# A first stage rebuilt: modulation on two engines, squares summed on TensorE

## The chip, the core and the metric

The kernel runs on one core of a Trainium2 chip. A core has TensorE (PE, matrix products; its weight loads are listed apart as PEld), VectorE (DVE), ScalarE (ACT), GpSimd (POOL) and SyncE (SP), which issues the loads. SBUF is the working memory, PSUM takes the matrix products. The metric is the device time of one execution in microseconds (us): 1756.03 us, the median of 3 runs (1755.61 to 1757.57).

## The reference

Two transformer-like blocks follow each other over 512 tokens of 1024 features. The change lies in the very first lines of the first block, the modulated norm and the projection behind it:

```python
c_act = jax.nn.silu(c)                               # c: one row of 1024
mod = c_act @ w_ada + b_ada                          # 1024 -> 3 x 1024
shift, scale, gate = jnp.split(mod, 3, axis=-1)
h = rms_norm(x, norm_in_gain) * (1.0 + scale) + shift
proj = h @ w_in                                      # q, k, v, z_attn, xbc, dt, z_ssm
```

rms_norm divides each token by the root of the mean of its squared features (plus 1e-6) and multiplies with a gain for each feature. Behind it come stick-breaking attention, a causal convolution with silu over the channels xbc, a chunked state-space scan, an out-projection scaled by gate, then a feed-forward layer, retention and pooling, a second feed-forward layer and a last norm. Nothing of these is touched, except that the weights for gate come under another name.

## The kernel before

Activations lie feature-major: a tile holds 128 features on the partitions and 512 tokens along the free axis, so x is eight tiles x0[0..7], and k counts the blocks of 128 features. A large product is taken as three float32r passes over operands split exactly in two, h and l: W.h times x.h, W.l times x.h, W.h times x.l. A float32r matmul with 512 columns is one instruction. A plain float32 matmul, as in the sums of columns, is two instructions.

TensorE's instructions run in the order in which the program writes them (`manual_schedule`). The other engines' order is made by a planner, which places an instruction where its inputs are ready by its own estimate; where the kernel wants another order, it adds a dependence with `after(later, earlier)`. All loads are issued by SP, in a single queue: a load that waits for a buffer holds those behind it.

The first stage, lines 313 to 400, does this:

- Loads (L344 to L350): x0[0], x0[1], the row c, x0[2..7], the vector table vec, the table cm. Then the rows of w_ada for shift and scale, 512 KB each for each k, and the first projection's weights wst[k], 384 KB each. For k above 0 these loads carry a dependence on the last square.
- Squares and their sum (L362 to L376): ACT squares each x0[k]. DVE adds the eight squares up. TensorE sums over the partitions with four matmuls of one column each (`colsum`, L252). DVE and POOL take the root, `rc` (L376); `bcast` (L272) spreads it as a row over all partitions: DVE makes a diagonal `dg`, TensorE multiplies it with ones into `Rp` in PSUM.
- silu(c): the row c is spread over the partitions by two matmuls with one row (L359), and ACT takes silu from PSUM into `cact`.
- Modulation (L322 to L342): for each k, shift and scale are two DVE instructions of 1024 elements that multiply 128 rows of w_ada with `cact` and sum up. `sh` and `gs` are made from these by two narrow ones.
- The loop over k (L383 to L400): POOL multiplies x0[k] with Rb, the copy of Rp in SBUF. ACT makes `hxh` with scale gs and bias sh. DVE makes the same in full precision (L395) and subtracts for `hxl` (L113). The weights are split by ACT (L132) and POOL (L133; for k = 1 DVE). TensorE multiplies six blocks in three passes, 18 matmuls for each k, into six PSUM banks `start_ps`.
- `warmup(n)` (L315) issues n matmuls of ones into a bank that nobody reads: 12 at the start, 10 behind silu's broadcasts, 11 behind the column sums, 6 behind Rp.

Behind the loop a queue of projections (`adv`) keeps TensorE fed with the remaining products on hx; the convolution takes `start_ps`.

Of the kernel before, what the change touches and what calls it, by code (L numbers as in the profile page):

```python
# [30 lines left out]
# columns of the vector table  # L31
# [3 lines left out]
def _vec_layout():  # L35
    n = 0
    for name, w in (
        ("gin", 8), ("bsh", 8), ("bsc", 8), ("bgt", 8), ("cw0", 12), ("cw1", 12), ("cw2", 12),
        ("cw3", 12), ("cb", 12), ("sbg", 8), ("ssg", 8), ("gf", 8), ("g1", 8), ("gm", 8), ("gb0", 8),
        ("gb1", 8), ("ps", 8), ("g2", 8), ("gfin", 8), ("dtb", 16), ("alog", 16), ("dsk", 16),  # L40
    ):
        VEC[name] = (n, w)
        n += w
    return n
# [5 lines left out]
def program(tc, A, out):  # L50
    """Activations lie feature-major [128 features, 512 tokens]; every large product is taken as three
    float32r passes over operands split exactly in two (h + l). TensorE runs in program order: `adv`
    interleaves the queue of projections with the products of attention, SSD and retention."""
# [71 lines left out]
    def wload(ap, n, dep=None, order=None, eng=None):  # L125
        r = wr.tile([P, 1024], F32, tag="wr", name=nm("wr"))
        d = SP.dma_start(r[:, :n], ap)
        if dep is not None:
            after(d, dep)
        h = wh.tile([P, 1024], F32R, tag="wh", name=nm("wh"))  # L130
        l = wl.tile([P, 1024], F32R, tag="wl", name=nm("wl"))
        i = ACT.copy(h[:, :n], r[:, :n])  # L132
        j = (eng or DVE).tensor_sub(l[:, :n], r[:, :n], h[:, :n].bitcast(F32))  # L133
        if order is not None:
            after(i, order[0])
            after(j, order[1])
        return h, l

    class Stream:
        """A projection's weights, in chunks of eight 128 x 128 blocks in the order of their use."""  # L140
# [16 lines left out]
    # ---------------------------------------------------------------- the queue of projections  # L157
# [6 lines left out]
    def adv(n=10**9):  # L164
        """Emit about n k-steps of the queued projections; the next one's first weights are asked for early."""
        while n > 0 and queue:
            job = queue[0]
            try:
                n -= next(job.steps)
            except StopIteration:  # L170
                queue.popleft()
                continue
            job.left -= 1
            if job.left == AHEAD and len(queue) > 1:
                queue[1].ahead()
# [9 lines left out]
    def proj(stream, xs, fin):  # L185
        """[128 features, 512 tokens] = stream's next blocks x xs."""
# [16 lines left out]
    def modeb(aps, n, xs, fin, side=None):  # L203
        """Token-major product: 4 banks [128 tokens, n]; aps: per pair of k-tiles [128, 2 * n]."""
# [30 lines left out]
    # ---------------------------------------------------------------- constants  # L235
# [16 lines left out]
    def colsum(sq, more=None, cols=range(4), pc=None):  # L252
        """sums over features, as columns of tokens"""
# [18 lines left out]
    def bcast(col, order=None, copies=1):  # L272
        """columns of tokens as a row on every partition (in PSUM)"""
# [38 lines left out]
    # ---------------------------------------------------------------- first block: modulated norm  # L312
    warm = ps_("warm")

    def warmup(n):  # L315
        """keeps TensorE's clock up while the first operands are made"""
# [4 lines left out]

    def matvec(src, col, dep=None, pool=(wr, "wr")):  # L322
        """col = rows of src (128 features x 1024) times silu(c)"""
        w = pool[0].tile([P, D], F32, tag=pool[1], name=nm("wa"))
        d = SP.dma_start(w, src)
        if dep is not None:
            after(d, dep)
        return DVE.scalar_tensor_tensor(w, w, 1.0, cact, op0=ALU.mult, op1=ALU.mult, accum_out=col)  # L328

# [3 lines left out]
    scaled = {}  # L333

    def modulation(k, dep=None, order=None):
        first = matvec(A["ada"][0, k], mv[:, k : k + 1], dep)
        second = matvec(A["ada"][1, k], mv[:, 8 + k : 9 + k], dep, (wh, "wh"))
        if order is not None:
            after(first if k else second, order)
        DVE.tensor_add(sh[:, k : k + 1], mv[:, k : k + 1], V("bsh", k))  # L340
        scaled[k] = DVE.scalar_tensor_tensor(gs[:, k : k + 1], mv[:, 8 + k : 9 + k], bsc1[:, k : k + 1], V("gin", k), op0=ALU.add, op1=ALU.mult)
        return first, second  # L342

    x0 = [a(F32, "x") for _ in range(KD)]  # L344
    for k in range(KD):
        SP.dma_start(x0[k], A["xT"][k])
        if k == 1:
            SP.dma_start(crow, A["c"])
    SP.dma_start(vec, A["vec"])
    SP.dma_start(cm, A["cm"])  # L350
    # one table for silu, square and copies
# [3 lines left out]
    cact = const([P, D], "cact")  # L355
    silus = []
    for n in range(2):
        pb = ps_("pb")
        mm(pb, ones[0:1, :], crow[:, 512 * n : 512 * n + 512], True, True)  # L359
        silus.append(ACT.activation(cact[:, 512 * n : 512 * n + 512], pb, AF.Silu))  # L360
    warmup(WARM[1])
    sq = None  # L362
    for k in range(KD):
        s = k_(F32, "sq")
        last = ACT.activation(s, x0[k], AF.Square)
        if k == 7:
            for i in silus:
                after(i, last)
        sq = accum(sq, s)
    DVE.tensor_scalar(bsc1, V("bsc"), 1.0, None, op0=ALU.add)  # L370
    pc = colsum(sq)
    warmup(WARM[2])
    rt = small([P, 4], "rct")
    order = DVE.tensor_scalar(rt, pc, 1.0 / D, EPS, op0=ALU.mult, op1=ALU.add)
    rc = small([P, 4], "rc")
    POOL.tensor_tensor(rc, rt, mhalf, op=ALU.pow)  # L376
    Rp = bcast(rc, modulation(0, order=order))
    scaled0 = DVE.tensor_tensor(x0[0], x0[0], Rp, op=ALU.mult)
    Rb = a(F32, "rb")
    after(ACT.copy(Rb, Rp), scaled0)  # L380
    warmup(WARM[3])
    hx = []
    start_ps = [ps_("mp") for _ in range(6)]  # L383
    for k in range(KD):
        dep = last if k > 0 else None
        if k > 0:
            modulation(k, dep, order[1] if k == 1 else scaled[1])
        h, l = a(F32R, "hxh"), a(F32R, "hxl")
        gk, sk = gs[:, k : k + 1], sh[:, k : k + 1]
        if k > 0:  # L390
            POOL.tensor_tensor(x0[k], x0[k], Rb, op=ALU.mult)
        i = ACT.activation(h, x0[k], AF.Identity, bias=sk, scale=gk)  # L392
        if k == 0:
            order = (i, scaled0)
        DVE.tensor_scalar(x0[k], x0[k], gk, sk, op0=ALU.mult, op1=ALU.add)  # L395
        lo(l, x0[k], h)
        hx.append((h, l))
        w = wload(A["wst"][k], 768, dep, (order[0], scaled[k]) if k else None, POOL if k != 1 else DVE)
        for n, (i, j) in enumerate(((0, 0), (1, 0), (0, 1))):
            for m in range(6):  # L400
                mm(start_ps[m], w[i][:, m * P : (m + 1) * P], hx[k][j], k == 0 and n == 0, k == KD - 1 and n == 2)

    # ---------------------------------------------------------------- conv + silu of the SSM channels
# [17 lines left out]
    # ---------------------------------------------------------------- z_ssm and dt, token-major  # L421
# [19 lines left out]
    # values of the attention, token-major, head by head as [h | l]  # L441
    VS = [[None] * 4 for _ in range(4)]

    def gate_part(m):
        """the gate of the first block, one eighth at a time"""
        matvec(A["ada"][2, m], mv[:, 16 + m : 17 + m])
# [13 lines left out]
    # queries and keys of the attention: a head's q as [h; l] on the partitions, k as [h; h] and [l; l]  # L460
# [45 lines left out]
    # softplus(x) = max(x, 0) + log1p(e), e = exp(-|x|); log1p(e) = 2 atanh(e / (2 + e))  # L506
# [24 lines left out]
    # cumulative log decay: as columns [token, (chunk, head)] and as rows, broadcast through DRAM  # L531
# [16 lines left out]
    # ---------------------------------------------------------------- SSD  # L548
# [11 lines left out]
    def post(c):  # L560
        """gate and normalise a finished chunk"""
# [103 lines left out]
    # the SSM half of the out-projection: x + gate * (W^T y), kept in DRAM during the attention  # L665
# [13 lines left out]
    # ---------------------------------------------------------------- attention  # L679
# [104 lines left out]
    # ---------------------------------------------------------------- out-projection of the first block  # L784
# [44 lines left out]
    # ---------------------------------------------------------------- feed-forward  # L829
    ff = {}  # L830

    def ffn(xs, win, wout, norm, gnext, last=False):
        """res += 0.5 * swiglu(R * xs); norm(n) gives R in two steps; the squares and split input of the next norm."""
# [64 lines left out]
    # ---------------------------------------------------------------- mixing: retention and pooling  # L898
# [112 lines left out]
    # pooled windows (feature-major, along the tokens)  # L1011
# [3 lines left out]
    def pool_fin(ps, g):  # L1015
# [8 lines left out]
        # the first windows are shorter: their count is t + 1  # L1024
# [76 lines left out]
    # ---------------------------------------------------------------- last rows and final norm, in two halves of the tokens  # L1101
# [8 lines left out]
    def rows(hf, hook=None):  # L1110
        """the last 256 features of half the tokens, and their squares"""
# [46 lines left out]
    def others(i, k):  # L1158
        """the sums of the features before, while the first half runs"""
# [4 lines left out]
    def first(i, k):  # L1164
        """the first half's norm and output, while the second runs"""
# [131 lines left out]
```

## Time and profile before

| | |
|---|---|
| median of 3 runs | 1756.03 us |
| profiled execution | span 1756.9 us |
| granted TensorE clock, mean | 0.991 |
| PE busy | 1720.6 us, 98% |
| DVE / ACT / POOL busy | 980.6 / 662.5 / 206.0 us |
| DMA, HBM read | 174.93 MB |

The profile is one execution, taken by the hardware profiler. Times are from the first instruction. In a list of groups, a row has the line, the engine, the operation, out<-in by the program's names, the shapes and the count, then the busy time in us and the mean of one in ns, then the idle time of the engine just before, with what ended it. In order of time, a row has its start, its length, and what it is. In a table of stretches, a row has the busy time of PE, PEld, DVE, ACT and POOL with the count of instructions, then PEclk, the share of the clock that TensorE was granted, the DMA engines' share and GB/s.

### The profile page before, as it was taken

What the parts mean: (1) busy time and instruction counts of PE and PEld (TensorE: products, weight loads), DVE (VectorE), ACT (ScalarE), POOL (GpSimd) and SP (SyncE); (2) the same over time, 40 slices, a digit from 0 to 9 for tenths busy, and PEclk for the clock granted to TensorE, in tenths of its full rate; (3) what the DMA queues carried; (4) which work ended last, traced back from release to release, by engine and by line L of the source; (5) the groups of instructions that cost most, each with busy time, mean ns of one, the idle gap of its engine ahead of it and who ended that gap; (6) DMA issues with size and microseconds to landing.
All of it is one profiled execution on the core that took longest, in us unless ns stands there. A gap on an engine that the chain in (4) does not pass through costs nothing.

```text
span 1756.9 us, 20492 instructions
## 1 busy us (share of the span) xinstructions
PE 1720.6 (98%) x8034; PEld 1432.1 (82%) x8034; DVE 980.6 (56%) x1347; ACT 662.5 (38%) x1023; POOL 206.0 (12%) x250
## 2 busy tenths in 40 slices
PE   8999899999999999999999999999999999999998
PEld 6798688777877888888888888888888888888887
DVE  7956965999967334333443636762544433433334
ACT  3545553667644222222333333332433322222232
POOL 4202212344321000000000000220000100000001
PEclk8999999999999999999999999999999999999999
DMA  6536344111132223222342222222223322222221
GB/s 231 183 89 201 96 156 156 61 61 60 56 116 94 97 99 104 95 98 96 120 132 90 85 90 90 78 97 96 96 96 114 102 96 96 96 96 96 96 96 49
DMA packets 56627, 182.59 MB, mean 104 GB/s; under 512 B 6289, under 2 KB 6609, under 8 KB 56530
## 3 DMA queue, kind: packets, MB, share of 16 engines
q1 hardware_dynamic: 56530, 181.28, 31.2%
q8 instruction: 63, 1.03, 0.2%
q14 instruction: 34, 0.28, 0.1%
HBM read 174.93 MB, written 6.32 MB: 103 GB/s over the span
## 4 chain that ended last, share of the span: by engine, by line
PE 82%; DVE 9%; issue 5%; POOL 2%; ACT 1%; DMA 1%; SPq 0%; POOLq 0%; DVEq 0%; ACTq 0%
PE mp L98 69%; PE mb L98 9%; DVE wa L328 1%; DVE om L725 1%; PE sc L98 1%; POOL be L723 1%; DVE wl L133 1%; PE ro L98 1%; POOL om L723 1%; DVE be L726 1%; PE yp L98 1%; DVE KL L113 1%; DVE x L395 1%; DVE wTl L113 0%; PE pc L98 0%
## 5 line engine op out<-in xcount | busy, mean ns | idle before, releaser
L132 ACT CAST wh<-wr 128x1024 fp32r<-128x1024 f32 (+3 forms) x288 | 298.0, 1036 | 779.0 <-PE mp L98 465.0
L133 DVE TENSOR_TENSOR wl<-wr,wh 128x1024 fp32r<-128x1024 f32 (+3 forms) x281 | 343.1, 1222 | 154.2 <-PE mp L98 86.2
L98 PE MATMUL mp<-xsh,wh 128*128 128x512 f32 x1024 | 401.3, 392 | 3.2 <-ACT xsh L109 3.2
L98 PE MATMUL mp<-xsl,wh 128*128 128x512 f32 x1024 | 399.2, 390 | 0.1
L98 PE MATMUL mp<-xsh,wl 128*128 128x512 f32 x1024 | 399.1, 390 | 0.0
L98 PEld LDWEIGHTS mp<-xsh,wh 128*128 128x128 f32 x1024 | 192.6, 188 | 43.2 <-ACT xsh L109 3.7
L98 PEld LDWEIGHTS mp<-xsl,wh 128*128 128x128 f32 x1024 | 192.7, 188 | 40.6 <-DVE xsl L114 0.6
L98 PEld LDWEIGHTS mp<-xsh,wl 128*128 128x128 f32 x1024 | 192.5, 188 | 40.4
L98 PE MATMUL mp<-aah,wh 128*128 128x512 f32 (+1 forms) x374 | 141.2, 377 | 0.0
L98 PE MATMUL mp<-aah,wl 128*128 128x512 f32 (+1 forms) x374 | 140.8, 377 | 0.0
L98 PE MATMUL mp<-aal,wh 128*128 128x512 f32 (+1 forms) x374 | 140.8, 376 | 0.0
L849 DVE TENSOR_TENSOR g<-g,mp 128x512 f32<-128x512 f32 x44 | 30.3, 688 | 155.4 <-PE mp L98 153.4
L98 PE MATMUL mp<-hxh,wh 128*128 128x512 f32 x288 | 112.5, 414 | 4.5 <-ACT hxh L392 4.5
L98 PE MATMUL mp<-hxh,wl 128*128 128x512 f32 x288 | 108.6, 400 | 0.8 <-POOL wl L133 0.8
L98 PE MATMUL mp<-hxl,wh 128*128 128x512 f32 x288 | 107.6, 396 | 1.0 <-DVE hxl L113 0.9
L309 POOL TENSOR_TENSOR ssq<-sq,sq 128x512 f32<-128x512 f32 x6 | 9.0, 1506 | 825.2 <-ACT sq L300 811.9
L847 DVE TENSOR_TENSOR g<-mp,rb 128x512 f32<-128x512 f32 x44 | 30.4, 692 | 118.4 <-PE mp L98 118.0
L98 PEld LDWEIGHTS mp<-aal,wh 128*128 128x128 f32 x374 | 70.4, 188 | 13.0
L98 PEld LDWEIGHTS mp<-aah,wh 128*128 128x128 f32 x374 | 70.4, 188 | 12.9
L98 PEld LDWEIGHTS mp<-aah,wl 128*128 128x128 f32 x374 | 70.4, 188 | 12.8
L98 PEld LDWEIGHTS mp<-hxh,wh 128*128 128x128 f32 x288 | 55.1, 193 | 17.3 <-ACT hxh L392 6.8
L98 PEld LDWEIGHTS mp<-hxh,wl 128*128 128x128 f32 x288 | 55.0, 192 | 14.9 <-POOL wl L133 2.8
(294 smaller groups left out, 2778.5 us busy)
## 6 DMA issues: line engine op xcount, KB each, us to landing
wr<-in_f1i SPq DMA_DIRECT2D x44, 512.0 KB, 3.3
wr<-in_f2i SPq DMA_DIRECT2D x44, 512.0 KB, 3.3
wa<-in_ada SPq DMA_DIRECT2D x24, 512.0 KB, 4.6
wr<-in_w2g SPq DMA_DIRECT2D x24, 512.0 KB, 3.2
wr<-in_f1o SPq DMA_DIRECT2D x22, 512.0 KB, 3.3
wr<-in_f2o SPq DMA_DIRECT2D x22, 512.0 KB, 3.3
wr<-in_w2qk SPq DMA_DIRECT2D x16, 512.0 KB, 3.3
wr<-in_wv SPq DMA_DIRECT2D x8, 512.0 KB, 3.4
```

The lines of the kernel that those rows point to most:

```text
L98: PE.matmul(o, l, r, start=start, stop=stop)
L113: return DVE.tensor_sub(l, src, h.bitcast(F32))
L132: i = ACT.copy(h[:, :n], r[:, :n])
L133: j = (eng or DVE).tensor_sub(l[:, :n], r[:, :n], h[:, :n].bitcast(F32))
L309: eng.tensor_add(n, acc, t)
L328: return DVE.scalar_tensor_tensor(w, w, 1.0, cact, op0=ALU.mult, op1=ALU.mult, accum_out=col)
L395: DVE.tensor_scalar(x0[k], x0[k], gk, sk, op0=ALU.mult, op1=ALU.add)
L723: POOL.affine_select(d, d, pattern=[[-1, P]], compare_op=ALU.is_gt, fill=fill, base=0, channel_multiplier=1)
L725: DVE.tensor_tensor_scan(o, o, zcol.to_broadcast([P, n]), 1.0, op0=ALU.mult, op1=ALU.add)
L726: DVE.tensor_tensor(be[:, off : off + n - 1], be[:, off : off + n - 1], om[:, off + 1 : off + n], op=ALU.mult)
L847: DVE.tensor_mul(g, pg, ff["Rb"])
L849: DVE.tensor_mul(g, g, pu)
```

## The change

- The weights for shift (`adash`) are laid out on the host as 128 x 128 blocks, inputs on the partitions. For each k, TensorE multiplies eight blocks with `ccol`, silu(c) as eight columns of 128 (from a new entry `cc` of vec), into one column of a PSUM bank `msh`; DVE adds the bias from there. The eight matmuls are float32, 16 instructions. They stand on TensorE behind the first of the three passes of the step before.
- scale stays on DVE, one instruction of 1024 elements for each k, with `cact`.
- x0[k] is multiplied with gs and Rp by one DVE instruction that reads Rp from PSUM; the copy Rb and POOL's products go. ACT adds sh for `hxh`. DVE takes `hxl` as (t + sh) - hxh in one instruction.
- The weights' low halves are made by DVE for all k; POOL has no part in the loop.
- The squares are not added on DVE. ACT squares even k, DVE odd k, and TensorE sums each at once: four matmuls of one column for each k, into the same four columns of PSUM. Between squares 3 and 4 stand silu(c)'s two broadcasts; behind each of the squares 4 to 7 stand two warm-up matmuls, behind all of them ten. The warm-ups of 11 and 6 go.
- vec is loaded ahead of c and of x0[2]. The loads of step k + 2 stand in the program at step k, without dependences on the last square, as scale's 512 KB, shift's two halves of 256 KB and wst's 384 KB.

```diff
-    def wload(ap, n, dep=None, order=None, eng=None):
...
+    def wsplit(r, n):
         h = wh.tile([P, 1024], F32R, tag="wh", name=nm("wh"))
         l = wl.tile([P, 1024], F32R, tag="wl", name=nm("wl"))
...
+        ACT.copy(h[:, :n], r[:, :n])
+        DVE.tensor_sub(l[:, :n], r[:, :n], h[:, :n].bitcast(F32))
         return h, l
...
         if k == 1:
+            SP.dma_start(vec, A["vec"])
             SP.dma_start(crow, A["c"])
-    SP.dma_start(vec, A["vec"])
...
+    def square_of(k):
+        s = k_(F32, "sq")
+        if k % 2:
+            DVE.tensor_mul(s, x0[k], x0[k])
+        else:
+            ACT.activation(s, x0[k], AF.Square)
+        for j in range(4):
+            PE.matmul(
+                pc[:, j : j + 1], s[:, j * P : (j + 1) * P], ones[:, 0:1], start=k == 0 and j == 0, stop=k == KD - 1,
+                skip_group_check=True)
+    pc = ps_("pc")
+    for k in range(4):
+        square_of(k)
+    ACT.activation(ccol, V("cc"), AF.Silu)
     for n in range(2):
         pb = ps_("pb")
         mm(pb, ones[0:1, :], crow[:, 512 * n : 512 * n + 512], True, True)
-        silus.append(ACT.activation(cact[:, 512 * n : 512 * n + 512], pb, AF.Silu))
+        ACT.activation(cact[:, 512 * n : 512 * n + 512], pb, AF.Silu)
+    for k in range(4, KD):
+        square_of(k)
+        warmup(2)
+    DVE.tensor_scalar(bsc1, V("bsc"), 1.0, None, op0=ALU.add)
+    rc = rsq(pc[:, 0:4], 1.0 / D)
     warmup(WARM[1])
...
+    def loads(k):
+        sc = rows_of(A["adasc"][k])
+        ws = []
+        for half in range(2):
+            ws.append(a(F32, "ash"))
+            SP.dma_start(ws[-1], A["adash"][k, half])
+        r = wr.tile([P, 1024], F32, tag="wr", name=nm("wr"))
+        SP.dma_start(r[:, :768], A["wst"][k])
+        return sc, ws, r
+    def shift_of(k, ws):
+        for j in range(8):
+            mm(msh[:, k : k + 1], ws[j // 4][:, j % 4 * P : (j % 4 + 1) * P], ccol[:, j : j + 1], j == 0, j == 7)
+        DVE.tensor_add(sh[:, k : k + 1], msh[:, k : k + 1], V("bsh", k))
+    def scale_of(k, sc):
+        matvec(sc, mv[:, k : k + 1])
+        DVE.scalar_tensor_tensor(gs[:, k : k + 1], mv[:, k : k + 1], bsc1[:, k : k + 1], V("gin", k), op0=ALU.add, op1=ALU.mult)
+    loaded = [loads(0), loads(1)]
+    scale_of(0, loaded[0][0])
+    shift_of(0, loaded[0][1])
+    Rp = bcast(rc)
+    start_ps = [ps_("mp") for _ in range(6)]
     for k in range(KD):
...
-        modulation(k, dep, order[1] if k == 1 else scaled[1])
...
+        if k + 2 < KD:
+            loaded.append(loads(k + 2))
         h, l = a(F32R, "hxh"), a(F32R, "hxl")
-        gk, sk = gs[:, k : k + 1], sh[:, k : k + 1]
-        if k > 0:
-            POOL.tensor_tensor(x0[k], x0[k], Rb, op=ALU.mult)
-        i = ACT.activation(h, x0[k], AF.Identity, bias=sk, scale=gk)
...
-        DVE.tensor_scalar(x0[k], x0[k], gk, sk, op0=ALU.mult, op1=ALU.add)
-        lo(l, x0[k], h)
+        t = k_(F32, "xr")
+        DVE.scalar_tensor_tensor(t, x0[k], gs[:, k : k + 1], Rp, op0=ALU.mult, op1=ALU.mult)
+        ACT.activation(h, t, AF.Identity, bias=sh[:, k : k + 1])
+        w = wsplit(loaded[k][2], 768)
+        DVE.scalar_tensor_tensor(l, t, sh[:, k : k + 1], h.bitcast(F32), op0=ALU.add, op1=ALU.subtract)
         hx.append((h, l))
-        w = wload(A["wst"][k], 768, dep, (order[0], scaled[k]) if k else None, POOL if k != 1 else DVE)
+        if k + 1 < KD:
+            scale_of(k + 1, loaded[k + 1][0])
         for n, (i, j) in enumerate(((0, 0), (1, 0), (0, 1))):
             for m in range(6):
                 mm(start_ps[m], w[i][:, m * P : (m + 1) * P], hx[k][j], k == 0 and n == 0, k == KD - 1 and n == 2)
+            if n == 0 and k + 1 < KD:
+                shift_of(k + 1, loaded[k + 1][1])
```

More of the change, by code (lines that the diff above doesn't have):

```diff
@@ L40, in _vec_layout @@
         ("gb1", 8), ("ps", 8), ("g2", 8), ("gfin", 8), ("dtb", 16), ("alog", 16), ("dsk", 16),
+        ("cc", 8),
     ):
@@ L123, in split, with wload @@
         return h, l
-    def wload(ap, n, dep=None, order=None, eng=None):
[L126 to L129, printed above, removed]
+    def wsplit(r, n):
         h = wh.tile([P, 1024], F32R, tag="wh", name=nm("wh"))
         l = wl.tile([P, 1024], F32R, tag="wl", name=nm("wl"))
[L132 to L136, printed above, removed]
+        ACT.copy(h[:, :n], r[:, :n])
+        DVE.tensor_sub(l[:, :n], r[:, :n], h[:, :n].bitcast(F32))
         return h, l
+    def wload(ap, n):
+        r = wr.tile([P, 1024], F32, tag="wr", name=nm("wr"))
+        SP.dma_start(r[:, :n], ap)
+        return wsplit(r, n)
     class Stream:
@@ L320, in program, with matvec, rows_of @@
     bsc1 = const([P, 8], "bsc1")
[L322 to L328, printed above, removed]
     gs, sh, gate = const([P, 8], "gs"), const([P, 8], "sh"), const([P, 8], "gate")
     mv = const([P, 24], "mv")
[L333 to L342, printed above, removed]
+    def matvec(w, col):
+        return DVE.scalar_tensor_tensor(w, w, 1.0, cact, op0=ALU.mult, op1=ALU.mult, accum_out=col)
+    def rows_of(src):
+        w = wr.tile([P, D], F32, tag="wr", name=nm("wa"))
+        SP.dma_start(w, src)
+        return w
     x0 = [a(F32, "x") for _ in range(KD)]
@@ L354, in program @@
     warmup(WARM[0])
-    cact = const([P, D], "cact")
-    silus = []
+    cact, ccol = const([P, D], "cact"), const([P, 8], "ccol")
+    def square_of(k):
[12 more added lines that the diff above has]
+    ACT.activation(ccol, V("cc"), AF.Silu)
     for n in range(2):
@@ L359, in program @@
         mm(pb, ones[0:1, :], crow[:, 512 * n : 512 * n + 512], True, True)
-        silus.append(ACT.activation(cact[:, 512 * n : 512 * n + 512], pb, AF.Silu))
-    warmup(WARM[1])
-    sq = None
-    for k in range(KD):
[L364 to L385, printed above, removed]
-        if k > 0:
-            modulation(k, dep, order[1] if k == 1 else scaled[1])
-        h, l = a(F32R, "hxh"), a(F32R, "hxl")
-        gk, sk = gs[:, k : k + 1], sh[:, k : k + 1]
-        if k > 0:
-            POOL.tensor_tensor(x0[k], x0[k], Rb, op=ALU.mult)
-        i = ACT.activation(h, x0[k], AF.Identity, bias=sk, scale=gk)
-        if k == 0:
-            order = (i, scaled0)
-        DVE.tensor_scalar(x0[k], x0[k], gk, sk, op0=ALU.mult, op1=ALU.add)
-        lo(l, x0[k], h)
+        ACT.activation(cact[:, 512 * n : 512 * n + 512], pb, AF.Silu)
@@ new lines, in program @@
+    for k in range(4, KD):
[3 more added lines that the diff above has]
+    rc = rsq(pc[:, 0:4], 1.0 / D)
+    warmup(WARM[1])
+    msh = ps_("msh")
+    def loads(k):
[4 more added lines that the diff above has]
+            SP.dma_start(ws[-1], A["adash"][k, half])
+        r = wr.tile([P, 1024], F32, tag="wr", name=nm("wr"))
+        SP.dma_start(r[:, :768], A["wst"][k])
+        return sc, ws, r
@@ new lines, in program @@
+    shift_of(0, loaded[0][1])
+    Rp = bcast(rc)
+    start_ps = [ps_("mp") for _ in range(6)]
+    hx = []
+    for k in range(KD):
+        if k + 2 < KD:
+            loaded.append(loads(k + 2))
+        h, l = a(F32R, "hxh"), a(F32R, "hxl")
+        t = k_(F32, "xr")
[3 more added lines that the diff above has]
+        DVE.scalar_tensor_tensor(l, t, sh[:, k : k + 1], h.bitcast(F32), op0=ALU.add, op1=ALU.subtract)
@@ L444, in gate_part @@
     def gate_part(m):
-        matvec(A["ada"][2, m], mv[:, 16 + m : 17 + m])
+        matvec(rows_of(A["adagt"][m]), mv[:, 16 + m : 17 + m])
         if m == 7:
@@ L1242, in prepare @@
         "alog": rep(i["a_log"][0]), "dsk": rep(i["d_skip"][0]),
+        "cc": col(i["c"][0]),
     }
@@ L1246, in prepare @@
     o["c"] = np.ascontiguousarray(i["c"])
-    o["ada"] = np.ascontiguousarray(i["w_ada"][0].T).reshape(3, 8, P, D)
+    wa = i["w_ada"][0]
+    sh = wa[:, :D].reshape(2, 4, P, 8, P).transpose(3, 0, 2, 1, 4)
+    o["adash"] = np.ascontiguousarray(sh).reshape(8, 2, P, 4 * P)
+    o["adasc"], o["adagt"] = (np.ascontiguousarray(wa[:, n * D : (n + 1) * D].T).reshape(8, P, D) for n in (1, 2))
     w = i["w_in"][0]
```

## The prediction

> **What bounds the kernel now.** I read the page first: engine shares and the chain by engine. The kernel is one long TensorE (PE) program, so a change of the first stage is worth what it moves the moment from which PE runs without a break.
>
> ```profile
> span 1756.9 us, 20492 instructions
> PE 1720.6 (98%) x8034; PEld 1432.1 (82%) x8034; DVE 980.6 (56%) x1347; ACT 662.5 (38%) x1023; POOL 206.0 (12%) x250
> PE 82%; DVE 9%; issue 5%; POOL 2%; ACT 1%; DMA 1%; SPq 0%; POOLq 0%; DVEq 0%; ACTq 0%
> ```
>
> Second, the chain of waits over the first 130 us (start, length, what).
>
> ```profile
> 2.49 5.44 DMA x<-in_xT
> ...
> 12.54 1.07 PE pc L98 x8
> ...
> 13.95 1.87 POOL rc L376
> 15.85 2.30 DVE dg L276
> ...
> 62.33 37.06 PE mp L98 x162
> ```
>
> The front half goes from x's tiles over VectorE's (DVE's) sums to the column sum at 12.54, the root on GpSimd (POOL), the diagonal dg, and on to PE. From 62.33 the chain is PE alone; one matmul costs 37.06/162 = 0.229 us there, so the last 18 of the start product end at 62.33 + 18 x 0.229 = 66.45. That end is what the change moves, and I pass its shift through in full. Third, PE in order of time, and one stretch by engine:
>
> ```profile
> 21.42 1.65 PE L98 MATMUL mp<-hxh,wh 128*128 128x512 f32 x6 [0.77 <-ACT hxh L392]
> 28.83 2.93 PE L98 MATMUL mp<-hxh,wh 128*128 128x512 f32 x6 [2.62 <-ACT hxh L392]
> 41.75 1.66 PE L98 MATMUL mp<-hxh,wh 128*128 128x512 f32 x6 [0.30 <-ACT hxh L392]
> 62.33 1.67 PE L98 MATMUL mp<-hxh,wh 128*128 128x512 f32 x6 [0.24 <-ACT hxh L392]
> 40.00:50.00 10.00, 8.98 (x36) 6.18 (x35) 9.96 (x17) 3.25 (x4) 5.19 (x2) 1.00 0.74 269
> ```
>
> Steps k = 3 to 7 of the loop take (62.33 - 41.75)/4 = 5.15 us each; DVE is busy 9.96 of 10 there, so DVE sets the step, though PE's own 18 x 0.229 = 4.12 is not far below. The loop takes 66.45 - 21.42 = 45.0 us.
>
> **The change, part by part.** *Prices on PE.* Squares and shift are fp32 matmuls with one moving column; each matmul is two instructions, as the column sums show (4 matmuls, x8).
>
> ```profile
> 1739.46 0.95 PE L98 MATMUL pc<-ones,sq 128*128 128x1 f32 x8
> 1740.27 0.36 PE L98 MATMUL mp<-aah,wh 128*128 128x256 f32 x1
> ...
> 544.78 1.84 PE L98 MATMUL pc<-ones,ssq 128*128 128x1 f32 x16
> 546.48 0.49 PE L98 MATMUL mp<-xsh,wh 128*128 128x512 f32 x1
> ...
> 1.06 4.49 PE L98 MATMUL warm<-ones 128*128 128x128 f32 x24 [1.06 <-POOL zcol L250]
> 5.48 1.98 PE L98 MATMUL pb<-crow,ones 1*128 1x512 f32 x4
> 7.39 3.94 PEld L98 LDWEIGHTS warm<-ones 128*128 128x128 f32 x20 [0.76 <-issue]
> 18.19 1.13 PE L98 MATMUL pb<-dg,ones 128*128 128x512 f32 x2 [0.70 <-DVE dg L276]
> 19.15 1.31 PEld L98 LDWEIGHTS warm<-ones 128*128 128x128 f32 x11 [0.24 <-issue]
> L98 PEld LDWEIGHTS warm<-ones x102: 186/192/338, 1.1 to 1750.0; 128*128 128x128 f32 x102
> ```
>
> Four squares' matmuls cost 1740.27 - 1739.46 = 0.81 us (0.101 an instruction); a shift, 16 instructions, 546.48 - 544.78 = 1.70. A warm-up instruction costs 0.12 at full clock (1.31/11) and 0.197 at half (3.94/20, where the next fence shows 0.50). No row shows a one-column matmul at half clock: it lies between 0.101 and twice that. It is bound by its weight load, whose longest and shortest in the last row stand 338 to 186; I take 0.101 x 338/186 = 0.18.
>
> *In the loop* PE then has 8 x 4.12 + 7 x 1.70 = 44.9 us, against 45.0 before: the time DVE gives up is filled by the seven shifts. DVE falls behind PE:
>
> ```profile
> L410 DVE SCALAR_TENSOR_TENSOR xbc<-mp,vec,xbc 128x511 f32<-128x511 f32 (+2 forms) x36 | 24.8, 740 | 2.2 <-ACT xbc L408 2.1
> L328 DVE SCALAR_TENSOR_TENSOR wa<-wa,cact 128x1024 f32<-128x1024 f32 x16 | 21.7, 1353 | 0.0
> L133 DVE TENSOR_TENSOR wl<-wr,wh x15: 817/881/1226, 64.5 to 125.7; 128x692 fp32r<-128x692 f32 x8, 128x1024 fp32r<-128x1024 f32 x6, 128x696 fp32r<-128x696 f32 x1
> L392 ACT ACTIVATE hxh<-x,sh,gs 128x512 fp32r<-128x512 f32 x8 | 6.5, 816 | 26.7 <-DVE gs L341 26.7
> ```
>
> That fence's nearest rows give DVE 0.74 (xr, with PSUM) + 0.74 (l) + 0.96 (wl, 0.88 for 692 columns, widened to 768) + 1.35 + about 0.5 for three narrow ones = 4.3 us a step, under PE's 5.8. The new wait, h(k+1) on the shift, is covered: 6 matmuls 1.37 + shift 1.70 + 0.2 + h 0.82 = 4.1, while PE still has 12 matmuls, to 5.8. Without that cover the 1.7 us of slack turn into a stall. SP issues four loads a step instead of three, the bytes stay 1408 KB ((1024 + 1024 + 768) columns x 128 x 4); they wait for buffers that the scale two steps earlier and the weight split free.
>
> ```profile
> 7.95 3.25 ACT L365 ACTIVATE sq<-x 128x512 f32<-128x512 f32 x5 [1.54 <-DMA x<-in_xT]
> 14.80 0.83 ACT L132 CAST wh<-wr 128x768 fp32r<-128x768 f32 x1 [2.49 <-DMA wr<-in_wst]
> 12.00:14.00 2.00, 1.46 (x13) 1.46 (x14) 0.85 (x3) 0.31 (x1) 0.05 (x1) 1.00 1.01 409
> ```
>
> At 409 GB/s a step's loads take 3.5 us, hidden under 5.8. The first weights still land at 14.8, since the same bytes go ahead of them. vec (128 x 220 fp32, 110 KB) ahead of x3 delays it by 0.3 us: x3 at 8.2 instead of 7.95, its square on DVE at 8.9.
>
> *Before the loop* is the loss. PE keeps program order: 24 warm-ups (to 5.4, as the row at 1.06), squares 0 to 2, square 3 not before 8.9, then silu(c)'s two broadcasts, then squares 4 to 7 with 4 warm-up instructions behind each, 20 more, shift 0, and only then Rp's broadcast. Before, the 8 column-sum instructions came at 12.54 after DVE's adds, and nothing of this stood in the way. What clock does it run at? Windows 3.41 us apart, with PEclk third from the end and PE's busy time behind the length:
>
> ```profile
> 4.33:7.75 3.42, 3.42 (x18) 2.05 (x18) 1.39 (x2) 1.10 (x2) 0.00 (x0) 1.00 0.87 276
> 7.75:11.16 3.41, 3.41 (x19) 3.41 (x18) 2.24 (x4) 3.11 (x5) 0.00 (x0) 0.50 1.05 371
> 11.16:14.57 3.41, 2.38 (x21) 2.19 (x21) 2.27 (x6) 1.12 (x3) 0.62 (x1) 1.00 1.02 413
> 14.57:17.99 3.42, 2.92 (x15) 2.62 (x13) 2.69 (x4) 0.83 (x1) 3.02 (x2) 0.50 1.02 406
> 417.34:420.75 3.41, 1.68 (x14) 1.34 (x12) 3.28 (x7) 0.84 (x2) 0.03 (x1) 1.00 0.17 67
> 420.75:424.16 3.41, 3.41 (x20) 2.95 (x19) 2.82 (x5) 3.37 (x7) 1.30 (x1) 1.00 0.02 5
> 543.63:547.04 3.41, 3.41 (x24) 3.09 (x23) 0.48 (x2) 0.00 (x0) 1.03 (x1) 1.00 0.45 154
> 547.04:550.46 3.42, 3.42 (x16) 2.63 (x15) 2.10 (x7) 0.46 (x1) 1.01 (x1) 1.00 0.00 0
> ```
>
> Two windows lost the clock for the next one: 4.33, though PE was busy all through (mostly the one-row broadcasts), and 11.16, busy 2.38 (8 one-column matmuls among them). The window at 417 was less busy, 1.68, with matmuls of 128 and 512 columns alone, and the next one, 420.75, kept 1.00. So I read that one-row and one-column matmuls hardly count as activity. In the new order nearly all of 4.33 to 22 is such work: half clock from 7.75 on; warm-ups alone (the 7.75 window) bring it back.
>
> The walk: square 3, 8.9 + 8 x 0.18 = 10.3; broadcasts, 1.98 at full, some 3.6 at half: 13.9. A square with its warm-ups, 8 x 0.18 + 4 x 0.197 = 2.23; square 7 ends at 13.9 + 3 x 2.23 + 1.44 = 22.0. Warm-ups 24 x 0.197: 26.7. Shift 0: 8 instructions at half to the window's end at 28.2, 8 at full: 29.0. Rp's broadcast 1.13, xr 0.74, h 0.82 and 0.2 of hand-over: first start matmul at 31.9, against 21.42: +10.5. What is made shorter hides under this. dg and the root, with no POOL work of the loop beside them, should run as their later executions do,
>
> ```profile
> L276 DVE TENSOR_TENSOR dg<-cm,rc x5: 417/692/2290, 15.8 to 1749.9; 128x512 f32<-128x512 f32 x3, 128x256 f32<-128x256 f32 x2
> L269 POOL TENSOR_TENSOR rc<-rct,mhalf x2: 1020/1022/1024, 497.3 to 1390.6; 128x4 f32<-128x4 f32 x2
> ```
>
> which took 0.69 and 1.02 where the first took 2.29 and 1.87; so Rp's input is there 2.2 us after square 7, while PE is busy with warm-ups and shift for 7.0. cact (13.9 + two silus, bounded by h's 0.82 each) and the first scale (+1.35) are ready by 17. If the planner puts silu(c) ahead of square 4 on ScalarE, square 4 waits 1.3 us more; I leave it in the range.
>
> Sum: +10.5 before the loop; -0.1 in it; and the window 28.23 to 31.64, with a shift, one broadcast and a gap, costs the clock until 35.05, (35.05 - 31.9)/2 = +1.6. Together +12.0 on the span, 1768.9, so 1768 against the median 1756.0 (the profiled span is 0.9 above it). With one-column matmuls at 0.101 at half clock: square 7 ends at 13.3 + 4.8 + 0.8 = 18.9, the first start matmul comes at about 28, +6.5; at 0.202 and two windows lost it is +15.
>
> [...]
>
> **The rivals.** *The clock stays full* before the loop: square 3 at 9.7, broadcasts 11.7, three squares with warm-ups (0.81 + 0.48 each) and the last, 16.4, warm-ups 19.3, shift 21.0, broadcast, xr, h: 23.9. +2.5, and -0.1 in the loop: 1758.4, within 0.2%. For it: the warm-ups between squares. Against: the rows 4.33 and 11.16, and 4 warm-up instructions are 0.48 of each 1.29 us. Even here PE's queue is longer than the chain it replaces.
>
> *Faster:* the shift's weight loads slip under the wide matmuls' streaming, so that a shift costs far less than 1.70, and the clock stays full. At no cost the stage ends at 23.9 + 32.9 = 56.8: 1746.4. It decides below a shift of 0.9 us, since 23.9 + 32.9 + 7 x 0.9 = 63.1 is 3.4 ahead of 66.45. For it: DVE's load does fall. Against: 544.78, where 16 such instructions between wide matmuls took 1.70 in full.
>
> *The loop loses the clock too*, with half of each shift's window not counting: if every second window is at half, 44.9 us become some 60: 1783. Against: 543.63, a window with 16 one-column instructions and wide ones for the rest; the next one, 547.04, had 1.00.
>
> **How the numbers follow.** Forecast 1768 with 0.65 (its own range 1762 to 1771), full clock 1758.4 with 0.17, faster 0.10, the loop's clock 0.08. What a measurement here can tell from no change is about 0.2%, 3.5 us. So faster 0.10, same 0.17, slower 0.73. The range 1757 to 1772 takes in the full-clock case and both bounds of the unknown price but leaves out the faster case and the loop's.
>
> **What would show it.** Right: PEclk 0.50 in most of 7.8 to 25, the first mp matmul near 32, steps of 5.8 us with DVE idle a quarter of the time, POOL idle, the start product's end near 78. Wrong: full clock before 20, a first mp matmul before 24, or steps under 5 us.

## The result and the profile after

The changed kernel takes 1770.65 us, the median of 4 runs (1770.44 to 1773.47); the kernel before, run beside it, 1756.80 us, the median of 4 (1755.61 to 1758.13). The ratio is 1.008, its 95% interval 1.0068 to 1.0092: slower by 13.9 us where 12 had been forecast. The page of the profiled execution:

```profile
span 1768.8 us, 20782 instructions
PE 1735.6 (98%) x8200; PEld 1451.8 (82%) x8200; DVE 960.5 (54%) x1334; ACT 659.1 (37%) x1019; POOL 175.9 (10%) x236
PE 87%; DVE 6%; issue 4%; POOL 2%; ACT 1%; DMA 0%; POOLq 0%; DVEq 0%; ACTq 0%
```

DVE has 20 us less to do than before and POOL 30 us less, yet the span is 11.9 us longer: PE has 15 us more, and PE is now 87% of the chain (`issue` in the chain is time in which an engine waited for nothing that the profile shows). The chain over the first 130 us (start, length, what) is PE from the first warm-up to Rp's broadcast at 29.11; not a DMA, a square or the root stands in it:

```profile
1.06 5.08 PE warm L99 x24
6.14 3.93 PE pc L354 x32
10.07 3.70 PE pb L99 x4
13.77 1.80 PE pc L354 x8
...
21.75 1.50 PE pc L354 x8
23.25 4.18 PE warm L99 x24
27.43 1.68 PE msh L99 x16
29.11 0.98 PE pb L99 x2
...
37.54 0.16 DVE sh L389
...
38.49 1.66 PE mp L99 x6
40.15 1.68 PE msh L99 x16
41.83 4.20 PE mp L99 x18
```

The table of stretches (PE, PEld, DVE, ACT and POOL busy, then PEclk, DMA share, GB/s) shows at which clock it went. PE is busy in all of 8.97 to 26.04 and is granted 0.50 in all of it:

```profile
8.97:12.38 3.41, 3.41 (x9) 2.17 (x9) 1.32 (x2) 0.28 (x1) 0.00 (x0) 0.50 1.04 405
...
19.21:22.62 3.41, 3.41 (x17) 3.41 (x18) 0.00 (x0) 0.00 (x0) 0.00 (x0) 0.50 0.00 0
22.62:26.04 3.42, 3.42 (x17) 3.42 (x18) 1.56 (x3) 0.00 (x0) 1.01 (x1) 0.50 0.00 0
26.04:29.45 3.41, 3.41 (x29) 3.20 (x29) 0.81 (x4) 0.00 (x0) 0.00 (x0) 1.00 0.56 180
29.45:32.86 3.41, 1.82 (x7) 1.02 (x6) 2.75 (x4) 0.72 (x1) 0.00 (x0) 1.00 0.38 135
...
48.00:56.00 8.00, 8.00 (x45) 6.84 (x44) 5.88 (x10) 2.83 (x4) 0.00 (x0) 1.00 0.79 262
```

From 19.21 to 22.62 DVE, ACT and POOL do nothing at all, and no load runs: everything waits for PE. In the loop (last row) PE is busy all the time and DVE 5.88 of 8. PE in order of time gives the loop, and the row at 78.22, the first matmul behind the start product, marks its end:

```profile
31.67 1.65 PE L99 MATMUL mp<-hxh,wh 128*128 128x512 f32 x6 [1.59 <-ACT hxh L407]
38.49 1.66 PE L99 MATMUL mp<-hxh,wh 128*128 128x512 f32 x6 [0.61 <-ACT hxh L407]
44.50 1.52 PE L99 MATMUL mp<-hxh,wh 128*128 128x512 f32 x6
...
74.14 1.52 PE L99 MATMUL mp<-hxh,wh 128*128 128x512 f32 x6
78.22 0.39 PE L99 MATMUL mp<-hxh,wh 128*128 128x512 f32 x1
```

The same mark in the profile of before:

```profile
66.59 0.39 PE L98 MATMUL mp<-hxh,wh 128*128 128x512 f32 x1
```

So the 11.9 us of the span are: first start matmul 31.67 - 21.42 = +10.25; start product (78.22 - 31.67) - (66.59 - 21.42) = +1.38; everything behind it +0.27.

### The profile page after: what moved, and what is told of

Same layout as the page of the kernel before. It is cut to its first block, busy times and chain, and to the rows that moved or that the text cites. A ratio compares the mean times of both kernels' runs of the same rounds, so it can differ in the third digit from the quotient of the medians.

```text
span 1768.8 us, 20782 instructions
## 1 busy us (share of the span) xinstructions
PE 1735.6 (98%) x8200; PEld 1451.8 (82%) x8200; DVE 960.5 (54%) x1334; ACT 659.1 (37%) x1019; POOL 175.9 (10%) x236
## 4 chain that ended last, share of the span: by engine, by line
PE 87%; DVE 6%; issue 4%; POOL 2%; ACT 1%; DMA 0%; POOLq 0%; DVEq 0%; ACTq 0%
PE mp L99 71%; PE mb L99 9%; PE sc L99 1%; PE ro L99 1%; PE warm L99 1%; DVE om L741 1%; DVE wl L130 1%; POOL om L739 1%; PE msh L99 1%; POOL be L739 1%; PE pb L99 1%; PE pc L354 1%; PE yp L99 1%; DVE be L742 1%; DVE KL L114 0%
## 5 line engine op out<-in xcount | busy, mean ns | idle before, releaser
L130 DVE TENSOR_TENSOR wl<-wr,wh 128x1024 fp32r<-128x1024 f32 (+3 forms) x288 | 349.1, 1213 | 157.9 <-PE mp L99 86.5
L99 PEld LDWEIGHTS mp<-hxl,wh 128*128 128x128 f32 x288 | 54.6, 189 | 10.6 <-issue 0.8
```

Of the source, the lines that this page charges most:

```text
L99: PE.matmul(o, l, r, start=start, stop=stop)
L130: DVE.tensor_sub(l[:, :n], r[:, :n], h[:, :n].bitcast(F32))
```

## The experiments

The theory from here on has two parts. The front is slow since PE, in program order, runs one-column and one-row work there, at a granted clock of 0.50 from 8.97 to 26.04. And the loop has become bound by PE, which has the shift to do. Rivals: it is the length of PE's queue, whatever the clock; or it is one of the two moves alone. The table gives each run's median, its ratio to the kernel before on the same chip, and two readings of its profile: the first start matmul, and the mark behind the start product. These two are read from one execution of each kernel.

| kernel | squares' sums | shift | median us | ratio (95%) | first | mark |
|---|---|---|---|---|---|---|
| before | DVE | DVE | 1756.8 | 1 | 21.42 | 66.59 |
| after | PE, 1 column | PE | 1770.65 | 1.0080 (1.0068 to 1.0092) | 31.67 | 78.22 |
| e1 | PE, 128 columns | PE | 1764.88 | 1.0039 (1.0024 to 1.0054) | 26.94 | 72.64 |
| e2 | DVE | PE | 1762.59 | 1.0030 (1.0014 to 1.0046) | 23.87 | 70.87 |
| e3 | as after, no last warm-ups | PE | 1772.11 | 1.0081 (1.0066 to 1.0096) | 31.10 | 78.23 |
| e4 | PE, 1 column | DVE | 1762.49 | 1.0028 (1.0018 to 1.0037) | 32.09 | 71.03 |
| e5 | as e1, broadcasts of 128 rows | PE | 1762.03 | 1.0030 (1.0018 to 1.0042) | 24.06 | 74.51 |
| e6 | new front | PE for 3 of 8 | 1748.29 | 0.9952 (0.9936 to 0.9967) | 20.25 | 57.75 |
| e7 | new front | PE | 1758.53 | 1.0012 (1.0002 to 1.0021) | 21.07 | 66.75 |
| e8 | new front | PE for 1 of 8 | 1749.59 | 0.9964 (0.9950 to 0.9979) | 20.03 | 59.79 |
| e9 | DVE | DVE | 1752.39 | 0.9971 (0.9959 to 0.9984) | 22.41 | 60.59 |
| e10 | as e6, one order tied | PE for 3 of 8 | 1747.70 | 0.9948 (0.9931 to 0.9965) | 20.14 | 56.85 |

### e1: the same number of instructions, 128 columns wide

```diff
-pc[:, j : j + 1], s[:, j * P : (j + 1) * P], ones[:, 0:1]
+pc[:, j * P : (j + 1) * P], s[:, j * P : (j + 1) * P], ones
...
-rc = rsq(pc[:, 0:4], 1.0 / D)
+rc = rsq(pc.rearrange("p (j t) -> p j t", j=4)[:, :, 0], 1.0 / D)
```

> The sums of squares read 128 columns of ones instead of one: as many instructions, the same weight loads, in the same place of PE's queue, only wider. Clock theory (one-column and one-row matmuls do not count as activity, so PE runs at half clock before the loop): the squares keep the clock, squares 4 to 7 with their warm-ups take some 5.5 us instead of 9.5 (13.8 to 23.3), and the first start matmul comes at 26 instead of 31.7: about 1765. Queue theory (the length of PE's queue alone is the loss): nothing shorter, 1770 to 1771. Shift theory (the shift's matmuls in the loop are the loss): 1770 to 1771.

The chain of e1, from square 3 on:

```profile
8.61 1.16 PE pc L354 x8
9.77 2.19 PE pb L99 x4
11.96 2.01 PE pc L354 x8
...
17.38 1.30 PE pc L354 x8
...
19.12 0.89 PE pc L354 x8
20.02 2.68 PE warm L99 x24
```

Each square's matmuls have 128 columns instead of one, and the front becomes 4.7 us shorter (26.94 against 31.67), the kernel some 6 to 7 us. Squares 0 to 3 now end at 9.77, still at full clock (PEclk 1.00 from 4.46 to 11.28). The half clock comes only behind the one-row broadcasts (0.50 from 11.28 to 18.11; 8 instructions 2.01) and is gone by the last square (1.00 from 18.11 to 21.52; 0.89). A queue of the same length at another clock gives another time, so the length alone is not it. The intervals of the two ratios do not overlap. The step of the loop stays at 5.93.

### e2: the squares' sums back on DVE

```diff
-        if k % 2:
-            DVE.tensor_mul(s, x0[k], x0[k])
...
+        ACT.activation(s, x0[k], AF.Square)
+        ssum0[0] = accum(ssum0[0], s)
...
+    rc = rsq(colsum(ssum0[0]), 1.0 / D)
```

> The squares' sums go back to VectorE (ScalarE squares all, VectorE adds, one column sum of 8 instructions behind the eight warm-ups); the rest as after. Clock theory and queue theory alike: 56 of 64 one-column instructions leave PE's queue, the column sum ends near 14, the first start matmul comes at 21 to 24, about 1761. Shift theory: the loop is as it was, at least 1768.

1762.59, first start matmul at 23.87: the front loses 7.8 us. The mark is still 4.28 behind before's: 2.45 of it at the first start matmul, where shift 0 stands on PE ahead of Rp's broadcast (2.09 us in e2's chain), and 1.83 in the start product, at 5.93 a step.

### e3: without the last ten warm-ups

```diff
     rc = rsq(pc[:, 0:4], 1.0 / D)
-    warmup(WARM[1])
```

> The ten warm-up matmuls (20 instructions) between the last square and shift 0 are left out. Queue theory: they stand in the way, without them Rp's broadcast comes 3.5 us earlier, 1767. Clock theory: they are what brings the clock back at 26; without them shift 0 runs at half (3.0 instead of 1.7), Rp's broadcast too (1.9 instead of 1.1), and the loop begins at half, which costs 1.5 to 3: 1769 to 1773. Shift theory: 1767 as the queue theory.

The chain of e3 behind square 7:

```profile
24.38 3.20 PE msh L99 x16
27.59 1.93 PE pb L99 x2
```

The ratio cannot be told from after's (1.0081 and 1.0080), and the mark is the same (78.23 and 78.22). The 20 warm-up instructions left out (after's group of 24 takes 4.18 us, some 3.5 of it theirs) give 0.57 us at the first start matmul, since shift 0 and the broadcast now run at half clock (PEclk 0.50 from 24 to 32; 3.20 and 1.93, where after has 1.68 and 0.98). Here the warm-ups pay for themselves, no more, and the queue theory, which wanted 1767, falls.

### e4: the shift's product back on DVE

```diff
+        ws = wh.tile([P, D], F32, tag="wh", name=nm("was"))
+        SP.dma_start(ws, A["adashr"][k])
...
-        for j in range(8):
-            mm(msh[:, k : k + 1], ws[j // 4][:, j % 4 * P : (j % 4 + 1) * P], ccol[:, j : j + 1], j == 0, j == 7)
+        matvec(ws, mv[:, 8 + k : 9 + k])
```

> The shift's product goes back to VectorE, one more instruction of 1024 elements a step, its rows loaded whole; PE has no shift. Shift theory: back to about 1757. Clock and queue theory: before the loop only shift 0 goes (1.7), in the loop DVE with 4.1 + 1.3 us a step sets the pace instead of PE's 5.9, some 3 us less over eight steps: about 1766.

The front stays (32.09): the 1.7 us that shift 0 was to give back there did not come. Square 7 ends at 23.87 instead of 23.25, the 24 warm-up instructions take 4.97 us instead of 4.18, and PE waits 2.39 us instead of 1.59 for its first product, now for the first weights' cast on ACT. The gain is in the loop, 38.9 us instead of 46.6, more than twice what the clock theory expected; the time lies between the two expectations. A stretch of it, and its last step:

```profile
50.00:60.00 10.00, 9.76 (x43) 7.72 (x42) 10.00 (x20) 4.05 (x6) 0.00 (x0) 1.00 0.91 300
```

```profile
39.08 1.52 PE L99 MATMUL mp<-hxh,wh 128*128 128x512 f32 x6
...
66.80 1.66 PE L99 MATMUL mp<-hxh,wh 128*128 128x512 f32 x6 [1.31 <-ACT hxh L403]
```

DVE is busy all the time, as before the change, but a step takes (66.80 - 39.08)/6 = 4.62 us, less than the 5.15 of before and the 5.93 of after. The loop without the shift on PE is faster than both.

### e9: both back on DVE

The edits of e2 and e4 together. What is left of the change is the fused products, POOL out of the loop, Rp read from PSUM and the order of loads.

> e2 and e4 together: the squares' sums and the shift's product both back on VectorE, the rest as after (fused products with silu(c), gain and scale from PSUM, order of loads). Theory (two separate losses that add, about 8 us each in e2 and e4): about 1753 to 1755, under before's 1757: first start matmul at 21 to 23, loop of 38 to 40 us. Rival (the two share one loss, or VectorE, which then has both jobs, gives one of them back): 1758 to 1761, as e2 or e4 alone.

PE in order of time in e9:

```profile
30.29 1.52 PE L99 MATMUL mp<-hxh,wh 128*128 128x512 f32 x6
...
56.37 1.66 PE L99 MATMUL mp<-hxh,wh 128*128 128x512 f32 x6 [1.14 <-ACT hxh L397]
...
60.59 0.39 PE L99 MATMUL mp<-hxh,wh 128*128 128x512 f32 x1
```

The two losses add. By the ratios the sums on PE cost 0.50% with the shift on PE (after and e2) and 0.57% without it (e4 and e9); the shift on PE costs 0.52% (after and e4) and 0.59% (e2 and e9): some 9 to 10 us each, to within about 3 by the intervals. The rest of the change gains 0.29%, about 5 us: steps of (56.37 - 30.29)/6 = 4.35 us, the mark at 60.59 instead of 66.59. (The profiled execution of e9 took 1749.29; its runs lie between 1748.88 and 1754.98.)

### e5: the broadcasts with 128 rows

```diff
-    crow = const([1, D], "crow")
+    crow = const([P, D], "crow")
+    DVE.memset(crow, 0.0)
...
-mm(pb, ones[0:1, :], crow[:, 512 * n : 512 * n + 512], True, True)
+mm(pb, ones, crow[:, 512 * n : 512 * n + 512], True, True)
```

> As e1 (squares' sums with 128 columns), and silu(c)'s broadcasts with 128 rows of which 127 are zero, in place of one row: same instructions, same count. Theory (a TensorE instruction of one row, like one of one column, does not count as work for the clock): the half clock that e1 kept from the broadcasts to about 17.5 us goes, squares 4 to 7 take 0.9 a group, square 7 ends near 16.5, the first start matmul at about 24 (26.94 in e1), some 1762. Rival (only the one column mattered, the half clock of e1 behind the broadcasts had another cause): as e1, first start matmul at 27 and 1765. Both keep loop steps of 5.9.

The chain, and two stretches behind it:

```profile
10.51 1.72 PE pb L99 x4
12.22 0.89 PE pc L355 x8
...
16.24 0.89 PE pc L355 x8
...
19.82 1.68 PE msh L99 x16
21.50 0.98 PE pb L99 x2
...
24.06 2.75 PE mp L99 x6
26.81 3.21 PE msh L99 x16
```

```profile
20.88:24.29 3.41, 1.81 (x9) 0.99 (x9) 2.43 (x7) 1.01 (x2) 0.00 (x0) 1.00 0.75 235
24.29:27.70 3.41, 3.41 (x12) 2.84 (x12) 2.29 (x4) 0.44 (x1) 0.00 (x0) 0.50 0.90 312
```

The expectation holds for the front: same instructions, 127 rows of zeros added, and no half clock from 8 to 24 (PEclk 1.00 in both stretches of 8 us), so one row does matter here. The median is the expected one (some 1762), but the interval overlaps e1's, so the time by itself does not tell the two apart. In the profiled execution the clock was lost later, 0.50 from 24.29 to 34.53, and the mark (74.51) lies behind e1's (72.64): there a front that is 2.9 us shorter was paid back in the first step. That execution took 1765.37 at a mean granted clock of 0.993; the other six took 1760.46 to 1764.57 at 0.995 to 0.997. So the loss in the first step is shown for this one execution; that the others kept the clock there is likely, but not shown.

### e6, e7, e8 and e10: another front

All four have the sums with 128 columns, all squares first, no warm-ups between or behind them, silu(c) from a c that the load brings on 128 partitions (512 KB instead of the broadcasts), and six warm-ups behind Rp's broadcast. The weights of shift 0 are loaded ahead of c, and row 0's first weights are split ahead of its hxh in the program. They differ in the rows k whose shift is on PE: 0, 1 and 4 in e6 and e10, all in e7, 0 alone in e8. e10 also ties one order.

```diff
-    for k in range(4):
+    for k in range(KD):
         square_of(k)
...
-        mm(pb, ones[0:1, :], crow[:, 512 * n : 512 * n + 512], True, True)
...
+    ACT.activation(cact, crow, AF.Silu)
...
+    ON_PE = (0, 1, 4)
...
+        if k not in ON_PE:
+            matvec(loaded[k][1], mv[:, 8 + k : 9 + k])
```

and in e10

```diff
-        ACT.activation(h, t, AF.Identity, bias=sh[:, k : k + 1])
+        hi = ACT.activation(h, t, AF.Identity, bias=sh[:, k : k + 1])
+        if k == 0:
+            after(hi, cast0[0])
```

> A front without the broadcasts (c arrives repeated on 128 partitions, 512 KB by DMA), all squares first, 128-column sums, no warm-ups between or behind them, six warm-ups behind the root's broadcast; the shift's product on TensorE for rows 0, 1 and 4, on VectorE for the other five. Theory (two separate losses, the front's half clock and the shift on TensorE at about 1.1 us a step over a VectorE step of 4.7): first start matmul at about 18, loop of 39 to 41 us, ends near 57 to 59 where after's ends at 78, so some 1747 to 1750: faster than both kernels. Rival (what the front gains is lost to weights that land late or to the clock): first start matmul later than 22 with waits on a DMA, 1753 or more.

> The same front as e6, the shift's product on TensorE for all eight rows, as in after. Theory: first start matmul near 18 and after's loop of 46 us, end of the start product near 64 to 65, some 1754 to 1756, level with before or a little under it. The difference to e6 and e8 is what the shift on TensorE costs in the loop: 6 to 8 us. Rival (the loop of after is long since the clock or the order at its start is disturbed by the front): a loop of 40 us or less here, 1748.

> The same front as e6, the shift's product on TensorE for row 0 alone, on VectorE for the other seven. Theory: VectorE sets the loop at 4.7 a step, so first start matmul near 18, a loop of 38 to 40 us, some 1746 to 1749, as e6 or up to 1 us from it. Rival (VectorE, which starts its products only after the root, is late from the first row on): steps over 5 us at the start, 1750 to 1753.

> e6 with ScalarE's order at the first row tied: the first weights' cast ahead of the first hxh, so that the low parts of row 0 are ready earlier. Theory (in e6 VectorE waits 0.63 us for that cast and this wait is on the path to row 1): 0.5 to 1 us off e6, some 1747.5. Rival (weights of row 1 or TensorE set row 1 anyway): as e6 within 0.5.

e6 is faster than both kernels (0.9952); e10, with the first weights' cast ahead of the first hxh, has its mark 0.9 us earlier, but the two intervals overlap. The first start matmul came at 20 to 21 instead of the expected 18. In e6 PEclk is 0.79 from 16 to 24, behind shift 0 (1.70 us from 13.87 on) and the wait for dg (0.87 us): by estimate, (1 - 0.79) x 8 / 0.5, some 3.4 us at half clock. The six warm-ups, 12 instructions from 17.73 to 20.25, take 0.21 us an instruction, where e5's 24 at full clock take 2.68, 0.11 each. In e10, where the first cast is out of the way, it is these warm-ups that stand in the chain right before the first start matmul (2.56 us from 17.92 on). In e7 another cause comes in, as ScalarE shows in order of time:

```profile
15.19 0.83 ACT L129 CAST wh<-wr 128x768 fp32r<-128x768 f32 x1 [1.09 <-DMA wr<-in_wst]
19.56 0.83 ACT L129 CAST wh<-wr 128x768 fp32r<-128x768 f32 x1 [3.53 <-DMA wr<-in_wst]
20.29 0.72 ACT L419 ACTIVATE hxh<-xr,sh 128x512 fp32r<-128x512 f32 x1
```

The planner put the cast of row 1's weights ahead of row 0's hxh, and this cast waited for its load until 19.56; hxh stood behind it. That is a part of the 2.5 us by which e7 (1758.53) missed the upper end of its 1754 to 1756. Its loop, 66.75 - 21.07 = 45.7 us, is after's (46.55) at another front, while e6 needs 57.75 - 20.25 = 37.5 and e8 39.8: the shift on PE for all rows costs 6 to 8 us in the loop, as expected. With one row only, DVE is late and waits for its loads (e8's chain has 6.01 us for one tile of scale's rows). e8's time lies just above its expected 1746 to 1749 and just under its rival's range. e6's mark is 2 us earlier than e8's; the intervals of their times overlap.

## Why the prediction was right, and where not

- **What bounds.** The premise, that the start product's end passes in full into the time, holds for this change: +11.63 at the mark, +11.9 in the span. In the other runs the span follows the mark within 2.2 us, in e9 within 3.4 (mark 6.0 earlier, span 1747.5 against 1756.9).
- **The front at half clock.** Forecast first start matmul 31.9, measured 31.67. e1 and e5 show the cause that was only read from two windows then: wider instructions, same count, and the clock stays, in e1 up to the one-row broadcasts and again from the last square on (1.00 to 11.28 and from 18.11 on), in e5 through the whole front (1.00 from 8 to 24). e5 also measures the walk of the rival with full clock (time 1758.4): it had the first start matmul at 23.9, and e5 has it at 24.06. So of the +10.25 some 7.6 are the clock, and 2.6 are the longer queue. The half clock needed no idle PE here: in after PE is busy 3.41 of 3.41 and the clock at 0.50 in five windows running. The half clock also came behind a window in which PE was mostly idle: before lost it behind this one, busy 1.40 of 3.42 with wide matmuls alone, and ran 28.23 to 35.05 of its own loop at 0.50.

```profile
24.81:28.23 3.42, 1.40 (x6) 0.79 (x5) 3.29 (x4) 0.27 (x1) 3.42 (x3) 1.00 0.03 11
```

- **One column at half clock.** Taken as 0.18 us an instruction, measured 1.50/8 = 0.188; a group with its four warm-up instructions 2.56 instead of 2.23, most of it in the warm-ups (1.06 instead of 0.79). Square 7 ended at 23.25 instead of 22.0.
- **x3 arriving late.** Wrong: DVE squared x3 from 7.13 on, not from 8.9. It did not show, since the 32 instructions of squares 0 to 3 were PE's own bound, 3.93 us, to 10.07 (forecast 10.3).
- **The warm-ups behind the squares.** The walk kept the half clock to 28.2 and had shift 0 end at 29.0; the clock came back at 26.04 and shift 0 ended at 29.11. Two errors of some 1.2 us, square 7 late and the clock early, cancelled by luck.
- **Root and dg hidden.** Right: they ran at 23.60 and 24.64, while PE did the warm-ups and the shift. The first scale, forecast by 17, ran only at 25.25 behind dg, still ahead of Rp's broadcast.

```profile
23.60 1.01 POOL L268 TENSOR_TENSOR rc<-rct,mhalf 128x4 f32<-128x4 f32 x1 [22.52 <-DVE rct L266]
```

- **The loop, -0.1.** This term failed. A step takes 5.93 us, not 5.8: behind a shift the 18 matmuls take 4.25 us, not 4.12 (7 times 0.13 = 0.9; why, no run shows). And between the first two steps PE waits: the steps start at 31.67 and 38.49, 6.82 apart, 0.9 more than the steps behind. The new wait, h(k + 1) on the shift, had been costed as covered, by PE's time. DVE's order was not looked at: the planner put the narrow addition for sh(1) behind the scale of row 2, its gain and xr of row 2.

```profile
35.36 1.22 DVE L325 SCALAR_TENSOR_TENSOR wa<-wa,cact 128x1024 f32<-128x1024 f32 x1
...
36.87 0.75 DVE L406 SCALAR_TENSOR_TENSOR xr<-x,gs,pb 128x512 f32<-128x512 f32 x1
37.54 0.15 DVE L389 TENSOR_TENSOR sh<-msh,vec 128x1 f32<-128x1 f32 x1
```

- **One more window at half clock, +1.6.** Wrong: PEclk is 1.00 from 26.04 on. The forecast counted windows of 3.41 us on from before's 7.75 and had one begin at 28.23; that this count carries over to another execution was the author's estimate, and no run shows the term. In after the clock changes at 8.97 and 26.04, five times 3.41 apart, so that the windows, counted on from there, begin at 26.04 and 29.45. The window from 29.45 holds 0.64 us of the broadcast and 1.19 us of wide matmuls, and the clock stayed (1.00 to 78). In e5 nearly the same stretch, cut at 20.88, holds 0.62 us of one-column shift, 0.98 of broadcast and 0.23 of wide matmuls, and the clock was lost for 10 us (0.50 from 24.29 to 34.53). Within each trace the changes of the clock named here lie multiples of 3.41 us apart, but they come at other times in each: at 7.75, 11.16, 28.23 and 35.05 in before, 8.97 and 26.04 in after, 11.28 and 18.11 in e1, 24.29 and 34.53 in e5. So this term could not be taken from before's profile, and belonged in the range; how much of it is chance from one execution to the next, no run shows.

The sum came out at 12.0 against 11.9 since the loop's loss (+1.38, forecast as -0.1) took the place of a window that was not lost (1.6): the reading of the front was right (31.67 against 31.9), the closeness of the sum is luck. The time missed 1768 by 2.6 us for another reason, which is no term of the sum: the forecast took the time to be 0.9 under the span, and in after it is 1.7 above the span of the same execution (1770.51 and 1768.8). In the other runs before's time is 1.7 to 1.8 above its span too, so the execution whose span is 1756.9 took, by estimate, some 1758.6, longer than the median of 1756.8. The rival "the loop loses the clock too" fell (1.00 throughout); "faster, since the shift slips under the wide matmuls" fell too: the shift takes its full 1.68 in every step. What no part of the prediction saw is that the loop on DVE would have taken 4.4 to 4.6 us a step with the fused products: against that loop the shift on PE costs about 9 us, and the prediction, which compared with before's loop alone, put it at nothing.

## What to carry to other kernels

Work moved to the engine that runs without a break was paid here in that engine's time, 1.68 us a step for the shift, though the engine it left got a quarter of the loop free (DVE busy 5.88 of 8); compare with what the rest of the change would give without the move, not only with the kernel before. TensorE's instructions of one column had nearly the price of 128 columns here (8 in 0.81 us against 8 in 0.89), and the front made of them and of one-row ones ran at a clock of 0.50 from 8.97 to 26.04: widening them (first start matmul 4.7 us earlier in e1), or taking them out of the front (7.8 in e2), was worth more here than filling with warm-ups (the first start matmul is at 31.10 without the last ten in e3, at 31.67 with them). Where a change adds a narrow instruction that PE waits for, look at where the planner puts it on its engine.

## What the runs showed of the hardware

- A matmul instruction of one column with 128 columns of weights took nearly the same place in the queue as one of 128 columns: 8 in 0.81 us before at full clock (one column) and 8 in 0.89 in e1 (128 columns). A window of the wider ones and warm-ups kept the clock: e1's 4.46 to 7.87, busy 3.41 of 3.41, was followed by 1.00. One of the narrow ones, but for its first 0.4 us, did not: after's 5.56 to 8.97, busy 3.41 of 3.41, was followed by 0.50.
- Two windows at full clock differ in their wide work: 1.83 of 3.41 us was followed by 1.00 (after, 29.45), 1.21 by 0.50 (e5, 20.88). This is a reading of two windows, not a run made for it, and gives no limit. With wide matmuls alone, 1.68 of 3.41 us was followed by 1.00 (417.34 in before) and 1.40 of 3.42 by 0.50 (24.81 in before).
- The broadcasts in e5 have 127 rows of zeros in the moving operand (and 128 rows of ones as weights) and kept the clock, 1.00 from 10.63 to 14.05 and in the window behind it, to 17.46. In e1, with one row, 0.50 followed from 11.28 to 18.11.
